# A host that lays x out feature-major and the small vectors as columns, so that the kernel loads x straight into h

## The chip, the cores and the metric

One Trainium2 chip, of which the kernel uses 1 core. The metric is the device time of one execution in microseconds, given as the median of several runs. Beside the timed runs there is one profiled execution, from which all rows below come.

## The reference, cut to what matters

Two transformer blocks run one after the other over 256 tokens of width 2048, all in float32. The first begins like this:

```python
def rmsnorm(x, g):
    x32 = x.astype(jnp.float32)
    y = x32 * lax.rsqrt(jnp.mean(x32 * x32, axis=-1, keepdims=True) + RMS_EPS)
    return (y * g.astype(jnp.float32)).astype(x.dtype)

h = x                                   # (1, 256, 2048)
hn = rmsnorm(h, mix_norm_g[0])
h = h + nsa_mixer(hn, ...)              # 2048 -> 5168 columns, three kinds of attention, 2048 -> 2048
h = h + swiglu(rmsnorm(h, ffn_norm_g[0]))
return rmsnorm(h, final_norm_g)
```

`nsa_mixer` multiplies the normed input by a 2048 x 5168 matrix, compresses keys and values with learned positions (`cmp_pos_k`, `cmp_pos_v`), attends, and projects back. The second block modulates its norms with `silu(c) @ w_mod + b_mod`, attends in two ways and ends in an MLP of width 8192. The norm's vectors, `c`, `b_mod` and the positions are short vectors; everything large is a weight matrix that is read once.

## The kernel before, in words

The residual stream is kept feature-major: tile `h` is 128 partitions x 16 feature blocks x 256 tokens (`KT` = 16, `S` = 256). A norm's 1/rms is a number for each token, so it is never applied to the input of a product: the product takes `x * g`, and its output is scaled by 1/rms when it leaves PSUM.

**Products.** Every float32 operand is split into two numbers of the fp32r type, hi (a rounded copy, ACT) and lo (the remainder, DVE), and each product is three matmuls: hi by hi (line 127), hi by lo (128), lo by hi (129). A `gemm` over 512 columns takes weights in pieces of two feature blocks by 512 columns (512 KB, tile `raw`, 5 buffers, loaded by SP's queue, line 93). ACT makes `whi` from it (line 84), DVE `wlo` (line 85), four buffers each; then TensorE has 24 matmuls of 256 columns on that piece, 12 for each feature block k. So a gemm over 16 blocks is 8 pieces and 192 matmuls. The accumulators are four PSUM banks, two for a gemm of 512 columns, so that the next gemm starts while the last one is being read out.

**Start.** `norm_x` (line 324) issues on SP's queue, in this order: the identity, `mix_norm_g`, and then x in 8 pieces of 256 features (256 KB each, tile `xt`, token-major) with 5 weight pieces among them: x0, w0, x1, w1, x2, x3, w2, x4, x5, w3, x6, x7, w4. Each x piece is turned by four TensorE transposes (line 341) into a PSUM bank; ACT writes `x` hi from that bank with the scale g (line 345), DVE the lo (346), and DVE copies the bank into `h` (348). The squares for the norm are taken from the token-major `xt` by 16 ACT instructions that sum along the row as they go (line 354), into `ssq`; a short DVE and ACT chain makes 1/rms of them (`rstd_x`, line 360). It is needed when the first gemm leaves PSUM (line 421). All other norms sum squares of `h`: `square_sums` (line 645) squares two feature blocks at once on ACT (653), adds them up in `sacc` on DVE (659; the first pair is written into `sacc` itself, the last pair stays in `slast`), and `rstd_col` (236) sums over partitions by six matmuls of one column (line 244). There is one buffer `slast`, so each square waits until DVE has added the one before.

**Vectors.** `columns` (line 218) loads short vectors as rows of 128 numbers and transposes them on TensorE (line 228) into columns, with a DVE copy out of PSUM. It is called for `mix_norm_g`, for seven vectors together (`vectors`, line 277), for the positions (414), and in `mod_cols` (1057) for the modulation and for `b_mod_2`.

**What sets the order.** A planner orders each engine's instructions by a simulated clock: at each point of it, it takes for an engine the ready instruction that comes first in the program. After that each engine runs its list strictly in order and waits at its head for what the next instruction needs. Dependencies are kept for the parts of a tile that an instruction touches. A generator (`self.inner`) emits the squares of `norm_x` one pair after each step of the first gemm, so in program order they stand after the work that feeds that step and before the weight split of the next.

The functions that the change touches:

Of the kernel before, what the change touches and what calls it, by code (L numbers as in the profile page):

```python
# [8 lines left out]
F32 = mybir.dt.float32  # L9
F32R = mybir.dt.float32r  # L10
AF = mybir.ActivationFunctionType
OP = mybir.AluOpType
AX = mybir.AxisListType
# [3 lines left out]
D = 2048  # L17
S = 256
KT = D // 128
# [3 lines left out]
EPS = 1e-6  # L23
# [43 lines left out]
class Kernel:  # L67
# [208 lines left out]

    def vectors(self):
        nc, a, m = self.nc, self.a, self.main
        vec1 = self.columns([(self.vec("ffn_norm_g", 16), 16), (self.vec("final_norm_g", 16), 16),
                             (self.vec("attn_norm_g_2", 16), 16), (self.vec("mlp_norm_g_2", 16), 16),  # L280
                             (self.vec("mla_q_norm_g_2", 3), 3), (self.vec("mla_kv_norm_g_2", 1), 1),
                             (self.vec("c_2", 16), 16)], "vec1")
        self.vecs = {"ffn": vec1[:, 0:16], "final": vec1[:, 16:32], "attn": vec1[:, 32:48],
                "mlp": vec1[:, 48:64], "lat": vec1[:, 64:68]}
        both = self.vecs["both"] = m.tile([128, 16], F32, name="both")
        t = m.tile([128, 16], F32, name="botht", tag="colb", bufs=1)
        nc.vector.tensor_tensor(t, vec1[:, 16:32], vec1[:, 16:32], OP.mult)
        nc.vector.tensor_scalar(t, t, EPS, None, op0=OP.add)
        nc.scalar.activation(both, t, AF.Sqrt)
        nc.vector.reciprocal(both, both)  # L290
        nc.vector.tensor_tensor(t, t, both, OP.mult)
        nc.vector.reciprocal(both, both)
        nc.vector.tensor_tensor(both, both, t, OP.add)
        nc.vector.tensor_scalar(both, both, 0.5, None, op0=OP.mult)
        csil = self.csil = m.tile([128, 16], F32, name="csil")
        nc.scalar.activation(csil, vec1[:, 68:84], AF.Silu)
        self.nsink = m.tile([128, 16], F32, name="nsink")
        nc.gpsimd.dma_start(self.nsink, self.src(a["swa_sinks_2"], 0, [[0, 128], [1, 16]]))
        nc.vector.tensor_scalar(self.nsink, self.nsink, -1.0, None, op0=OP.mult)
# [24 lines left out]
    def norm_x(self):  # L324

        nc, a = self.nc, self.a
        self.gmix = self.columns([(self.vec("mix_norm_g", 16), 16)], "gmix", nc.sync)
        xs = [self.pair("x") for _ in range(KT)]
        xt = []
        for s in range(8):  # L330
            xt.append(self.main.tile([128, 2, S], F32, name="xt", tag="u", bufs=16))
            nc.sync.dma_start(xt[s], self.src(a["x"], s * S, [[D, 128], [128 * D, 2], [1, S]]))
            if s in (0, 1, 3, 5, 7):
                self.ahead.append(self.raw_cols(a["nsa_w_in"], 5168, 256 * len(self.ahead), 2, [(2048, 512)]))
        banks = (("O", 1), ("PT", 1), ("S", 2), ("S", 2))
        for s in range(8):
            p = self.bank(*banks[s % 4])
            k = 2 * s
            for i in range(2):
                for t in range(2):  # L340
                    nc.tensor.transpose(p[:, i * S + t * 128:i * S + (t + 1) * 128],
                                        xt[s][:, t, i * 128:(i + 1) * 128], self.ident)
            for i in range(2):
                g, pi = self.gmix[:, k + i:k + i + 1], p[:, i * S:(i + 1) * S]
                nc.scalar.activation(xs[k + i][:, 0, :], pi, AF.Copy, scale=g)
                nc.vector.scalar_tensor_tensor(xs[k + i][:, 1, :], pi, g, xs[k + i][:, 0, :].bitcast(F32),
                                               op0=OP.mult, op1=OP.subtract)
            nc.vector.tensor_copy(self.h[:, k:k + 2, :].rearrange("p k n -> p (k n)"), p)
        ssq = self.main.tile([128, 2, 8], F32, name="ssq")

        def squares():
            for s in range(8):
                for t in range(2):
                    nc.scalar.activation(self.slast[:, t * S:(t + 1) * S], xt[s][:, t, :], AF.Square,
                                         accum_out=ssq[:, t, s:s + 1])
                yield
        self.inner = squares()
        return xs, ssq

    def rstd_x(self, ssq):  # L360
        for _ in self.inner:
            pass
        rc = self.main.tile([128, 2], F32, name="rc_x")
        self.nc.vector.tensor_reduce(rc, ssq, AX.X, OP.add)
        self.nc.vector.tensor_scalar(rc, rc, 1.0 / D, EPS, op0=OP.mult, op1=OP.add)
        return self.rsqrt(rc, self.main, "rcx")


    def bias_table(self, rel, which, pool):
# [26 lines left out]
    def nsa(self, xs, ssq, mp):  # L396
        nc, a, tc = self.nc, self.a, self.tc
        W, LD = a["nsa_w_in"], 5168
        with ExitStack() as es:
            p = es.enter_context(tc.tile_pool(name="attn", bufs=1))  # L400
# [9 lines left out]
            rc = None  # L410

            with tc.tile_pool(name="cmp", bufs=1) as cp:
                dtab = self.bias_table("rel_bias", 0, cp)
                pos = self.columns([(a["cmp_pos_k"].rearrange("a b c -> (a b) c"), 32),
                                    (a["cmp_pos_v"].rearrange("a b c -> (a b) c"), 32)], "pos")
                ku = cp.tile([128, 2, 32, 60], F32, name="ku")
                for ci in range(2):
                    t = cp.tile([128, 4, S], F32, name="kc", tag="kc", bufs=1)
# [40 lines left out]
                g = cp.tile([128, 2, 48], F32, name="g")  # L459
# [9 lines left out]
                for j, (t, br) in enumerate(((0, 1), (0, 2), (0, 0), (1, 0), (1, 1), (1, 2))):  # L469
                    s = g[:, t, br * 16:(br + 1) * 16]  # L470
# [192 lines left out]
    def sums(self, col, last=2):  # L663
        acc = self.sacc[:, :S]
        self.nc.vector.tensor_tensor(acc, acc, self.sacc[:, S:], OP.add)
        return [(acc, col)] + [(self.slast[:, i * S:(i + 1) * S], col) for i in range(last)]
# [390 lines left out]
    def mod_cols(self, o, n, name):  # L1057

        d = self.modv
        mv = self.columns([(bass.AP(tensor=d.tensor, offset=d.offset + 128 * o, ap=[[128, n], [1, 128]]), n)], name)  # L1060
        bv = self.columns([(self.vec("b_mod_2", n, 128 * o), n)], "b_")
        self.nc.vector.tensor_tensor(mv, mv, bv, OP.add)
        return mv

# [111 lines left out]
_SKIP = ("s5_A_re", "s5_A_im", "s5_log_dt", "s5_B_re", "s5_B_im", "s5_C_re", "s5_C_im", "s5_D", "s5_w_glu")  # L1176


# [13 lines left out]
```

## Time and profile before

| | us |
|---|---|
| median of 3 timed runs | 2123.52 |
| lowest and highest of them | 2122.17, 2125.51 |
| the profiled execution's own time | 2119.85 |
| its span, first to last instruction | 2118.0 |

The span holds 2094.1 us in which the profile counts TensorE (PE) as busy, 1452.0 us of DVE, 1017.1 us of ACT. The ends of matmuls are modelled, so how fast TensorE really goes is read from the distance between the starts of two matmuls, in the timeline.

### The profile page before, as it was taken

What the parts mean: (1) busy time and instruction counts of PE and PEld (TensorE: products, weight loads), DVE (VectorE), ACT (ScalarE), POOL (GpSimd) and SP (SyncE); (2) the same over time, 40 slices, a digit from 0 to 9 for tenths busy, and PEclk for the clock granted to TensorE, in tenths of its full rate; (3) what the DMA queues carried; (4) which work ended last, traced back from release to release, by engine and by line L of the source; (5) the groups of instructions that cost most, each with busy time, mean ns of one, the idle gap of its engine ahead of it and who ended that gap; (6) DMA issues with size and microseconds to landing.
All of it is one profiled execution on the core that took longest, in us unless ns stands there. A gap on an engine that the chain in (4) does not pass through costs nothing. (4 is left out here: it accounts for less than half of the span.)

```text
span 2118.0 us, 40943 instructions
## 1 busy us (share of the span) xinstructions
PE 2094.1 (99%) x16405; PEld 1992.5 (94%) x16405; DVE 1452.0 (69%) x2144; ACT 1017.1 (48%) x1504; POOL 162.9 (8%) x297
## 2 busy tenths in 40 slices
PE   9999999999999999999999999999999999999998
PEld 8899999999999999999999999899889989989987
DVE  7467876787777777877867676677676555555556
ACT  6334655554434434443445465565434534534543
POOL 2211000010110111101000000000100000000000
PEclk9999999999999999999999999999999999999999
DMA  8778555889889888888975663568887656656663
GB/s 277 261 234 311 170 163 180 286 265 296 276 282 303 274 301 281 279 294 276 298 233 156 182 183 112 160 196 280 283 294 233 194 191 194 193 193 193 192 194 133
DMA packets 288302, 492.29 MB, mean 232 GB/s; under 512 B 27111, under 2 KB 139338, under 8 KB 287856
## 3 DMA queue, kind: packets, MB, share of 16 engines
q1 hardware_dynamic: 254128, 371.20, 55.2%
q0 software_dynamic: 33408, 117.70, 16.7%
q8 instruction: 128, 2.10, 0.4%
q10 hardware_dynamic: 576, 0.79, 0.1%
q14 instruction: 62, 0.51, 0.1%
HBM read 487.21 MB, written 2.20 MB: 231 GB/s over the span
## 5 line engine op out<-in xcount | busy, mean ns | idle before, releaser
L84 ACT ACTIVATE whi<-raw 128x1024 fp32r<-128x1024 f32 (+2 forms) x716 | 746.2, 1044 | 904.8 <-PE acc L128 645.4
L85 DVE TENSOR_TENSOR wlo<-raw,whi 128x1024 fp32r<-128x1024 f32 (+2 forms) x716 | 853.5, 1200 | 392.1 <-ACT whi L84 378.8
L127 PE MATMUL acc<-x,whi 128*128 128x256 f32 x3184 | 882.6, 278 | 3.2 <-ACT v L463 1.4
L128 PE MATMUL acc<-x,whi 128*128 128x256 f32 x3184 | 884.3, 278 | 0.0
L129 PE MATMUL acc<-x,wlo 128*128 128x256 f32 x3184 | 882.7, 278 | 0.2 <-DVE wlo L85 0.2
L127 PEld LDWEIGHTS acc<-x,whi 128*128 128x128 f32 x3184 | 597.8, 188 | 8.6 <-issue 5.0
L128 PEld LDWEIGHTS acc<-x,whi 128*128 128x128 f32 x3184 | 599.4, 188 | 5.4 <-issue 4.6
L129 PEld LDWEIGHTS acc<-x,wlo 128*128 128x128 f32 x3184 | 599.0, 188 | 1.4 <-DVE wlo L85 0.6
L742 DVE SCALAR_TENSOR_TENSOR macc<-mw,csil,macc 128x1024 f32<-128x1024 f32 x180 | 231.1, 1284 | 175.0 <-DMA mw<-w_mod 174.1
L128 PE MATMUL acc<-u,whi 128*128 128x256 f32 x1260 | 349.7, 279 | 0.8 <-DVE u L85 0.8
L127 PE MATMUL acc<-u,whi 128*128 128x256 f32 x1260 | 346.3, 280 | 1.0 <-DVE h L642 0.6
L129 PE MATMUL acc<-u,wlo 128*128 128x256 f32 x1260 | 347.0, 278 | 0.0
L128 PEld LDWEIGHTS acc<-u,whi 128*128 128x128 f32 x1260 | 236.7, 188 | 1.9 <-DVE u L85 1.5
L127 PEld LDWEIGHTS acc<-u,whi 128*128 128x128 f32 x1260 | 234.9, 188 | 3.2 <-ACT u L84 1.0
L129 PEld LDWEIGHTS acc<-u,wlo 128*128 128x128 f32 x1260 | 235.9, 188 | 0.7 <-issue 0.2
L164 PE MATMUL acc<-whi,u 128*128 128x512 f32 (+1 forms) x544 | 206.2, 379 | 0.0
L165 PE MATMUL acc<-wlo,u 128*128 128x512 f32 (+1 forms) x544 | 206.1, 379 | 0.0
L163 PE MATMUL acc<-whi,u 128*128 128x512 f32 (+1 forms) x544 | 204.4, 376 | 0.0
L736 POOL DMA_DIRECT2D mw<-w_mod x192 | 102.6, 534 | 1003.2 <-PE acc L129 657.7
L164 PEld LDWEIGHTS acc<-whi,u 128*128 128x128 f32 x544 | 102.2, 188 | 20.6 <-issue 0.4
L163 PEld LDWEIGHTS acc<-whi,u 128*128 128x128 f32 x544 | 102.1, 188 | 20.3
L165 PEld LDWEIGHTS acc<-wlo,u 128*128 128x128 f32 x544 | 102.2, 188 | 18.4
(349 smaller groups left out, 1316.9 us busy)
## 6 DMA issues: line engine op xcount, KB each, us to landing
raw<-w_ff SPq DMA_DIRECT2D x256, 512.0 KB, 4.1
mw<-w_mod POOLq DMA_DIRECT2D x192, 512.0 KB, 5.6
raw<-ffn_w_in SPq DMA_DIRECT2D x352, 256.0 KB, 5.0
raw<-ffn_w_out SPq DMA_DIRECT2D x87, 512.0 KB, 5.3
raw<-nsa_w_in SPq DMA_DIRECT2D x72, 512.0 KB, 5.3
raw<-nsa_w_out SPq DMA_DIRECT2D x32, 512.0 KB, 4.5
raw<-w_out SPq DMA_DIRECT2D x32, 512.0 KB, 4.0
raw<-w_in SPq DMA_DIRECT2D x24, 512.0 KB, 3.9
```

What stands on the lines that cost most here:

```text
L84: self.nc.scalar.activation(hi, x, AF.Copy)
L85: self.nc.vector.tensor_tensor(lo, x, hi.bitcast(F32), OP.subtract)
L127: mm(out, wh, xh, start=first, stop=False, skip_group_check=True)
L128: mm(out, wh, xl, start=False, stop=False, skip_group_check=True)
L129: self.last = mm(out, wl, xh, start=False, stop=last, skip_group_check=True)
L163: mm(o, xt[:, 0, q], hi, start=k == 0, stop=False)
L164: mm(o, xt[:, 1, q], hi, start=False, stop=False)
L165: self.last = mm(o, xt[:, 0, q], lo, start=False, stop=k == nk - 1)
L736: ld = nc.gpsimd.dma_start(wt, self.src(self.a["w_mod_2"], k * 128 * LD + s * 1024, [[LD, 128], [1, 1024]]))
L742: nc.vector.scalar_tensor_tensor(acc, wt, csil[:, k:k + 1], acc, op0=OP.mult, op1=OP.add)
```

## The change

The host passes x transposed (`l_xT`, 2048 x 256), and the short vectors as matrices with 128 rows (`l_gmix`, `l_vec1`, `l_pos`, `l_bmod`). The kernel loads each with one DMA in the shape in which it is used. x goes into `h` in the same 8 pieces, on the same queue, in the same places among the weight pieces. ACT and DVE make x hi and lo from `h`, and the squares go through `square_sums` and `rstd_col`.

```diff
     def vectors(self):
-        vec1 = self.columns([(self.vec("ffn_norm_g", 16), 16), ... (self.vec("c_2", 16), 16)], "vec1")
+        vec1 = m.tile([128, 84], F32, name="vec1")
+        nc.gpsimd.dma_start(vec1, a["l_vec1"])
...
     def norm_x(self):
-        self.gmix = self.columns([(self.vec("mix_norm_g", 16), 16)], "gmix", nc.sync)
+        self.gmix = self.main.tile([128, 16], F32, name="gmix")
+        nc.sync.dma_start(self.gmix, a["l_gmix"])
         xs = [self.pair("x") for _ in range(KT)]
-        xt = []
         for s in range(8):
-            xt.append(self.main.tile([128, 2, S], F32, name="xt", tag="u", bufs=16))
-            nc.sync.dma_start(xt[s], self.src(a["x"], s * S, [[D, 128], [128 * D, 2], [1, S]]))
+            nc.sync.dma_start(self.h[:, 2 * s:2 * s + 2, :],
+                              self.src(a["l_xT"], 256 * s * S, [[S, 128], [128 * S, 2], [1, S]]))
             if s in (0, 1, 3, 5, 7):
                 self.ahead.append(self.raw_cols(a["nsa_w_in"], 5168, 256 * len(self.ahead), 2, [(2048, 512)]))
-        for s in range(8):
-            p = self.bank(*banks[s % 4])
...
-                    nc.tensor.transpose(p[:, i * S + t * 128:i * S + (t + 1) * 128],
-                                        xt[s][:, t, i * 128:(i + 1) * 128], self.ident)
...
-            nc.vector.tensor_copy(self.h[:, k:k + 2, :].rearrange("p k n -> p (k n)"), p)
+        for k in range(KT):
+            g, x = self.gmix[:, k:k + 1], self.h[:, k, :]
+            nc.scalar.activation(xs[k][:, 0, :], x, AF.Copy, scale=g)
+            nc.vector.scalar_tensor_tensor(xs[k][:, 1, :], x, g, xs[k][:, 0, :].bitcast(F32),
+                                           op0=OP.mult, op1=OP.subtract)
+        sums = self.square_sums()
         def squares():
-            for s in range(8):
-                for t in range(2):
-                    nc.scalar.activation(self.slast[:, t * S:(t + 1) * S], xt[s][:, t, :], AF.Square,
-                                         accum_out=ssq[:, t, s:s + 1])
+            for k in range(0, KT, 2):
+                sums(k)
                 yield
...
     def rstd_x(self, _):
         for _ in self.inner:
             pass
-        rc = self.main.tile([128, 2], F32, name="rc_x")
-        self.nc.vector.tensor_reduce(rc, ssq, AX.X, OP.add)
-        self.nc.vector.tensor_scalar(rc, rc, 1.0 / D, EPS, op0=OP.mult, op1=OP.add)
-        return self.rsqrt(rc, self.main, "rcx")
+        return self.rstd_col(self.sums(self.cD[:, 0:1]), EPS, self.main, "rcx")
...
-                pos = self.columns([(a["cmp_pos_k"]..., 32), (a["cmp_pos_v"]..., 32)], "pos")
+                pos = cp.tile([128, 64], F32, name="pos")
+                nc.gpsimd.dma_start(pos, a["l_pos"])
...
-        bv = self.columns([(self.vec("b_mod_2", n, 128 * o), n)], "b_")
+        bv = self.main.tile([128, n], F32, name="bv", tag="colb", bufs=1)
+        self.nc.gpsimd.dma_start(bv, self.a["l_bmod"][:, o:o + n])
```

## Rows read from the trace of the kernel before

**Rows 1.** The page's list of engines: busy us (share of the span), instructions.

```profile
PE 2094.1 (99%) x16405; PEld 1992.5 (94%) x16405; DVE 1452.0 (69%) x2144; ACT 1017.1 (48%) x1504; POOL 162.9 (8%) x297
```

**Rows 2.** Windows: length, busy PE, PEld, DVE, ACT, POOL; clock, DMA share, GB/s.

```profile
5.00:10.00 5.00, 2.02 (x12) 1.78 (x11) 2.79 (x5) 3.78 (x12) 2.48 (x6) 0.80 1.04 308
10.00:15.00 5.00, 5.00 (x39) 5.00 (x39) 2.72 (x4) 3.81 (x12) 1.97 (x4) 0.86 1.08 348
15.00:20.00 5.00, 5.00 (x46) 5.00 (x45) 4.06 (x7) 5.00 (x19) 0.00 (x0) 1.00 1.07 374
...
1150.00:1155.00 5.00, 2.25 (x10) 1.74 (x9) 3.25 (x11) 1.57 (x4) 0.00 (x0) 0.65 0.78 246
```

**Rows 3.** Timeline of PE, first products: start, us, instruction, [idle before].

```profile
8.41 1.12 PE L341 MATMUL PT<-ident,xt 128*128 128x128 f32 x4 [2.98 <-DMA xt<-x]
9.18 0.56 PE L127 MATMUL acc<-x,whi 128*128 128x256 f32 x1
...
9.76 0.41 PE L127 MATMUL acc<-x,whi 128*128 128x256 f32 x1
9.97 0.41 PE L128 MATMUL acc<-x,whi 128*128 128x256 f32 x1
...
13.86 0.36 PE L127 MATMUL acc<-x,whi 128*128 128x256 f32 x1
```

**Rows 4.** Timeline of ACT and DVE: splits of weight pieces 0, 1 and 4.

```profile
6.54 1.06 ACT L84 ACTIVATE whi<-raw 128x1024 fp32r<-128x1024 f32 x1 [0.52 <-DMA raw<-nsa_w_in]
11.03 1.06 ACT L84 ACTIVATE whi<-raw 128x1024 fp32r<-128x1024 f32 x1 [0.98 <-DMA raw<-nsa_w_in]
...
22.23 1.23 DVE L85 TENSOR_TENSOR wlo<-raw,whi 128x1024 fp32r<-128x1024 f32 x1 [0.31 <-ACT whi L84]
```

**Rows 5.** SP's timeline, and DMA issues (last column us to landing): pieces 2, 4.

```profile
4.73 0.92 SPq L93 DMA_DIRECT2D raw<-nsa_w_in  x1
raw<-nsa_w_in SPq DMA_DIRECT2D x1, 512.0 KB, 9.2
...
12.22 0.37 SPq L93 DMA_DIRECT2D raw<-nsa_w_in  x1
raw<-nsa_w_in SPq DMA_DIRECT2D x1, 512.0 KB, 7.5
```

**Rows 6.** Timeline of PE: one group of four transposes among matmuls.

```profile
15.00 0.28 PE L127 MATMUL acc<-x,whi 128*128 128x256 f32 x1
15.12 0.60 PE L341 MATMUL O<-ident,xt 128*128 128x128 f32 x4
15.48 0.37 PE L128 MATMUL acc<-x,whi 128*128 128x256 f32 x1
15.68 0.28 PE L129 MATMUL acc<-x,wlo 128*128 128x256 f32 x1
```

**Rows 7.** Groups by line, 0-45, then 366-446 us; ACT's waits, 360-450: us, times, longest.

```profile
L354 ACT ACTIVATE slast<-xt 128x256 f32<-128x256 f32 x16 | 6.5, 410 | 3.4 <-DMA xt<-x 3.4
L348 DVE COPY h<-S 128x512 f32<-128x512 f32 x4 | 2.7, 681 | 0.0
...
L653 ACT ACTIVATE slast<-h 128x512 f32<-128x512 f32 x7 | 4.4, 630 | 8.1 <-DVE h L642 4.1 <-DVE sacc L659 4.0
...
ACT slast L653 <- DVE sacc L659: 4.0, 4, 1.6
```

**Rows 8.** Timeline of PE: the one-column matmuls of a later norm.

```profile
440.00 0.28 PE L128 MATMUL acc<-x,whi 128*128 128x256 f32 x1
...
440.48 1.03 PE L244 MATMUL S<-cD,slast 128*128 128x1 f32 x8
441.37 0.36 PE L129 MATMUL acc<-x,wlo 128*128 128x256 f32 x1
```

**Rows 9.** Timeline of DVE in the projection after the first attention.

```profile
377.80 1.28 DVE L642 TENSOR_TENSOR h<-h,acc 128x512 f32<-128x512 f32 x2
379.00 0.48 DVE L673 SCALAR_TENSOR_TENSOR x<-h,vec,x 128x256 fp32r<-128x256 f32 x1
```

More of the change, by code (lines that the diff above doesn't have):

```diff
@@ L278, in vectors @@
         nc, a, m = self.nc, self.a, self.main
[L279 to L282, printed above, removed]
+        vec1 = m.tile([128, 84], F32, name="vec1")
+        nc.gpsimd.dma_start(vec1, a["l_vec1"])
         self.vecs = {"ffn": vec1[:, 0:16], "final": vec1[:, 16:32], "attn": vec1[:, 32:48],
@@ L333, in norm_x @@
             if s in (0, 1, 3, 5, 7):
                 self.ahead.append(self.raw_cols(a["nsa_w_in"], 5168, 256 * len(self.ahead), 2, [(2048, 512)]))
-        banks = (("O", 1), ("PT", 1), ("S", 2), ("S", 2))
-        for s in range(8):
-            p = self.bank(*banks[s % 4])
-            k = 2 * s
-            for i in range(2):
-                for t in range(2):
-                    nc.tensor.transpose(p[:, i * S + t * 128:i * S + (t + 1) * 128],
-                                        xt[s][:, t, i * 128:(i + 1) * 128], self.ident)
[L343 to L347, printed above, removed]
-            nc.vector.tensor_copy(self.h[:, k:k + 2, :].rearrange("p k n -> p (k n)"), p)
@@ L349, in norm_x @@
-        ssq = self.main.tile([128, 2, 8], F32, name="ssq")
+        for k in range(KT):
[4 more added lines that the diff above has]
+        sums = self.square_sums()
         def squares():
-            for s in range(8):
-                for t in range(2):
-                    nc.scalar.activation(self.slast[:, t * S:(t + 1) * S], xt[s][:, t, :], AF.Square,
-                                         accum_out=ssq[:, t, s:s + 1])
+            for k in range(0, KT, 2):
+                sums(k)
@@ L356, in squares, with rstd_x @@
                 yield
         self.inner = squares()
-        return xs, ssq
-    def rstd_x(self, ssq):
+        return xs, None
+    def rstd_x(self, _):
         for _ in self.inner:
             pass
-        rc = self.main.tile([128, 2], F32, name="rc_x")
-        self.nc.vector.tensor_reduce(rc, ssq, AX.X, OP.add)
-        self.nc.vector.tensor_scalar(rc, rc, 1.0 / D, EPS, op0=OP.mult, op1=OP.add)
-        return self.rsqrt(rc, self.main, "rcx")
+        return self.rstd_col(self.sums(self.cD[:, 0:1]), EPS, self.main, "rcx")
@@ L413, in nsa @@
                 dtab = self.bias_table("rel_bias", 0, cp)
-                pos = self.columns([(a["cmp_pos_k"].rearrange("a b c -> (a b) c"), 32),
-                                    (a["cmp_pos_v"].rearrange("a b c -> (a b) c"), 32)], "pos")
+                pos = cp.tile([128, 64], F32, name="pos")
+                nc.gpsimd.dma_start(pos, a["l_pos"])
                 ku = cp.tile([128, 2, 32, 60], F32, name="ku")
@@ L1176, with layouts, cols @@
 _SKIP = ("s5_A_re", "s5_A_im", "s5_log_dt", "s5_B_re", "s5_B_im", "s5_C_re", "s5_C_im", "s5_D", "s5_w_glu")
+def layouts(a):
+    def cols(*names):
+        return np.ascontiguousarray(np.concatenate([a.pop(n).reshape(-1, 128).T for n in names], 1))
+    return {"l_xT": np.ascontiguousarray(a.pop("x").reshape(S, D).T), "l_gmix": cols("mix_norm_g"),
+            "l_vec1": cols("ffn_norm_g", "final_norm_g", "attn_norm_g_2", "mlp_norm_g_2", "mla_q_norm_g_2",
+                           "mla_kv_norm_g_2", "c_2"),
+            "l_pos": cols("cmp_pos_k", "cmp_pos_v"),
+            "l_bmod": np.ascontiguousarray(a["b_mod_2"].reshape(-1, 128).T)}
 def kernel(**inputs):
@@ L1185 @@
     arrays.update(constants())
+    arrays.update(layouts(arrays))
     aps = {n: nc.dram_tensor(n, v.shape, mybir.dt.from_np(v.dtype), kind="ExternalInput").ap()
```

## The prediction

> **What bounds the kernel now.** I begin with the page's list of engines: PE counts as busy for 2094.1 of 2118.0 us, DVE for 69% and ACT for 48% [rows 1]. So only two things can move the time: work taken from or given to PE, and the few stretches in which PE is fed too slowly. The change touches the first 40 us, so the second view is the windows of the start: from 5 to 20 us the DMA share is above 1.0 (308 to 374 GB/s), and from 15 to 20 us ACT is full, 5.00 of 5.00 [rows 2]. The third is PE's timeline: it waited 2.98 us for the second x piece and began its first product at 9.18 us; up to about 11.4 us matmuls start 0.21 us apart (9.76, 9.97), later 0.12 (15.00, 15.12) [rows 3, 6]. The fourth is who feeds the products: ACT split weight piece 0 at 6.54 and piece 1 at 11.03, each time right after a wait for its DMA [rows 4]. So the start is set by DMA, ACT and PE in turn, and what a freed PE gains there must be held against when the pieces land.
>
> **What goes from PE.** 32 transposes of x in 8 groups of four. One group in the stream: the matmul at 15.00 is followed by the next at 15.48 and the second next at 15.68, where 0.12 apart would give 15.12 and 15.24, so a group costs 0.44 us [rows 6]. Two of the groups (the first at 4.8 us and the one at 8.41) stand in the start-up wait; two stand together just before 13.86, and four come after it (rows 6 show one of them). The four are worth 4 x 0.44 = 1.8 us; the rest is in the start below. The column transposes of `vec1`, `pos` and `b_mod` go too. At most each costs what a group of four costs (0.44), at least what one of four does (0.11); a single narrow transpose is nearest the lower end, so I take 0.15 each, 0.5 us, range 0.3 to 1.3. The one of `mix_norm_g` lies in the start-up wait and is worth nothing.
>
> **What comes to PE.** Six matmuls of one column, which the trace shows as 12 records: from 440.00 to 441.37 instead of 0.12 later, and the usual 0.08 behind it [rows 8, 6], that is 1.33 us, once, wherever the planner puts it. If they wait there for DVE's last sum, more; that is a rival below.
>
> **The start, step by step.** x0 and piece 0 land as before: the queue order is the same and the bytes are the same; `l_gmix` is the same 8 KB. Without transposes the first product needs x hi and `whi` 0 only: 6.54 + 1.06 = 7.60 us instead of 9.18 [rows 4, 3]. If the clock rises at the same moment, at 11.4, there are 3.8 / 0.21 = 18 matmuls by then and 6 more at 0.12, so the 24 of piece 0 are done at 12.1. Piece 1 lands at 11.03, its `whi` is ready at 12.1, its `wlo` 1.23 later at 13.3. So block 2 starts between 12.1 and 13.1 instead of 13.86 [rows 3, 4]: 0.8 to 1.8 us. Piece 2, issued at 4.73, lands at 13.9, piece 4 at 12.22 + 7.5 = 19.7 [rows 5]. From landing to `wlo` is 1.06 + 1.23 = 2.3 us, and the first matmul that needs it is the third, 0.2 us in: piece 4's block 8 can't go in full before 21.8. Where was it before? From 13.86, six blocks of 12 matmuls at 0.115 (the rows' 0.12, and 0.11 as often) are 8.3 us, four groups of transposes 1.8: 23.9 us, when `wlo` 4 had just been made (22.23 + 1.23 = 23.5 [rows 4]). PE alone would gain 0.8 to 1.8 plus 1.8, so 2.6 to 3.6 us; the landings allow 2.1; and if ACT and DVE hand over piece 4 no earlier than now, 0.4. After piece 4 there is no x left to load and weights come faster than PE eats them, so what is won at block 8 is kept.
>
> **Do ACT and DVE keep up?** ACT loses 16 squares, 6.5 us [rows 7], and gets 8 of 128x512 at 0.63, 5.0 us: 1.5 us less, and the x hi that now read SBUF stay as they are. DVE loses 8 copies of 128x512 at 0.68, 5.4 us, and gets 6 adds of the same shape, for which the copy is the nearest row, 4.1, and one half as wide, 0.4: 0.9 us less. Neither is more loaded. I therefore take the limit of the landings, 2.1 us, and keep 0.4 and 3.6 as ends. The `rstd` chain becomes longer, but 1/rms is wanted only when the first gemm leaves PSUM (13.86 + 14 x 12 x 0.115 + 1.8 = 35 us now), and the second gemm has two other banks and 192 x 0.115 = 22 us of work then: it costs nothing, and the cover is that second gemm.
>
> **The rest.** POOL issues two DMAs for nine in the first 13 us, and one for one near 1082 us; nothing on PE waits for these. The queue of SP has the same DMAs in the same order, so nothing is moved past anything. For `b_mod`, POOL loads it without waiting for PE, and the add that uses it waits for `modv` in any case.
>
> **The sum.** -2.1 - 0.5 + 1.3 = -1.3 us, against the profiled execution's span of 2118.0 (its own time is 2119.85, so 1.85 us lie outside the span and stay). The timed median lies 3.7 us above that execution; the same difference taken from it gives 2123.5 - 1.3 = 2122.2 us, 0.06% less. With the ends: -0.4 - 0.3 + 1.3 = +0.6 and -3.6 - 1.3 + 1.3 = -3.6 us, so 2119.9 to 2124.1 for this case alone. All of it lies within 0.2% (4.2 us), about what a measurement of this kernel can tell from no change.
>
> **Rivals.** *First, the faster one: PE alone sets the start, and the later stretches shift well too.* For it speaks that x lo and hi no longer queue behind transposes, so both engines can work ahead from the landings. It gives -3.6; and the order elsewhere changes, since the planner runs its clock anew. Near 1150 us PE works 2.25 of 5 us at a granted clock of 0.65 [rows 2]: 0.35 x 5 = 1.75 us are lost in that window alone, and a stretch like it may fall better. Together -5.3 us: 2118.2. Against it: piece 4's landing at 19.7.
>
> *Second, slower: squares and adds lock ACT and DVE together.* Each square after the second must wait until DVE has added the one before, as there is one `slast`. Four such waits cost ACT 4.0 us near 420 us [rows 7]. At the start ACT is full from 15 us and DVE nearly, and both run their lists in order; behind a waiting square stand x hi and the next weight split on ACT, for these DVE's lo parts wait, and for both PE. Six waits at 1.0 us are 6.0, less the 1.5 that ACT is relieved and the 0.4 by which `wlo` 4 was early: weight splits come 4.1 us later than now. PE's own savings then only lengthen its waits, and -0.5 + 1.3 stays: +4.9 us, 2128.4. It decides where more than about 2 us of these waits fall before piece 4's split; below that it eats only my gain. Against it: the planner knows the dependency and can put an add early; before, 16 squares stood in the same place.
>
> *Third, x does not come straight: products wait for all of `h`.* If a read of block 0 waited for all eight loads of `h`, the first product would start 9 us later. But DVE wrote two further pairs of `h` at 377.80 before it read the first pair at 379.00 [rows 9], though the program has them the other way round: parts of `h` are told apart. I give it 2%, in the slower share.
>
> *Fourth, the clock.* Until 9.18 PE now has transposes at 4.8 and 8.41 us; afterwards nothing between the warm-up and 7.6. In 5 to 10 us the granted clock is 0.80, in 10 to 15 us 0.86 [rows 2]: (0.20 + 0.14) x 5 / 0.5 = 3.4 us are already at the lower level (1.2 of 2.4 GHz). If the rise comes 2 us later than it does now, 9 matmuls take 0.1 us more each, 0.9 us, though partly under the wait for piece 1: the time is 2122.2 to 2123.1, still the same. The Trainium skill (TensorE: Matmul & The Clock Gate, Part 1: The HAM clock gate) says that the engine is throttled by default and only sustained activity releases it; by that rule the early idle stretch speaks against the change. The trace agrees so far, with 0.80 around the wait of 2.98 us.
>
> **How the numbers follow.** My forecast with the fourth rival 0.58, the first 0.22, the second with the third 0.20. Faster by over 0.2% is the first alone, slower the second and third. The range takes in both: 2117.0 to 2128.0.
>
> **What would show it.** First product at 7.6 to 8 us; block 2 near 13; no L341; 12 records of L244 before 40 us without idle time ahead of them; ACT's waits for L659 in 10 to 25 us below 2 us in all. I am wrong if PE shows waits for `whi` or `wlo` in 12 to 35 us, or waits at L244, or if the stretches near 1150 and 1268 us change by more than the start does.

## The result and the profile after

The changed kernel takes 2206.57 us (median of 4 runs, 2205.49 to 2209.33), the kernel before beside it 2124.52 (2122.17 to 2127.41): ratio 1.0391, 95% interval 1.0378 to 1.0404, some 82 us slower. The profiled execution took 2205.49 us, its span is 2203.7. No case of the prediction held this.

The first line to read is the list of engines, the answer to [rows 1]:

```profile
PE 2178.8 (99%) x16381; PEld 2069.6 (94%) x16381; DVE 1457.3 (66%) x2138; ACT 1012.8 (46%) x1479; POOL 159.2 (7%) x290
```

PE has 24 records fewer and is busy 84.7 us longer, at the same 99%. Its idle time hardly grows (23.9 us of the span before, 24.9 after), so the slowdown is not a wait: the work itself takes longer. A window from the middle of the kernel, which the change does not touch, shows it. First before, then after (columns as in [rows 2]):

```profile
700.00:1140.00 440.00, 439.61 (x3888) 436.72 (x3887) 327.06 (x346) 191.50 (x214) 41.11 (x79) 1.00 0.83 272
```

```profile
700.00:1140.00 440.00, 440.00 (x3679) 437.15 (x3678) 317.75 (x325) 176.74 (x191) 41.36 (x77) 1.00 0.84 268
```

In the same 440 us at the same granted clock PE goes through 209 matmuls fewer. The timeline of PE there, before and after (start, us, instruction):

```profile
900.04 0.28 PE L129 MATMUL acc<-x,wlo 128*128 128x256 f32 x1
900.15 0.28 PE L127 MATMUL acc<-x,whi 128*128 128x256 f32 x1
900.27 0.28 PE L128 MATMUL acc<-x,whi 128*128 128x256 f32 x1
900.38 0.28 PE L129 MATMUL acc<-x,wlo 128*128 128x256 f32 x1
```

```profile
900.04 0.28 PE L129 MATMUL acc<-x,wlo 128*128 128x256 f32 x1
900.16 0.28 PE L127 MATMUL acc<-x,whi 128*128 128x256 f32 x1
900.28 0.28 PE L128 MATMUL acc<-x,whi 128*128 128x256 f32 x1
900.40 0.28 PE L129 MATMUL acc<-x,wlo 128*128 128x256 f32 x1
```

Three steps take 0.34 us before and 0.36 after. Averaged over all neighbouring starts in the two traces (my own count, gaps over 150 ns left out), 256-column matmuls of lines 127 to 129 stand 113.9 ns apart before and 119.9 after. There are 13,332 of them: 6.0 ns each is 80 us. At the end of the first gemm the changed kernel is 1.6 us late, and 191 x 6.0 ns = 1.1 us of that is the new spacing already; so the start, on which nearly all of the prediction was spent, is worth little.

In the code of these matmuls nothing changed. What changed is where their operands lie. Each matmul has a moving operand, 256 columns of `x` or `u` (`u` holds the moving pairs of other gemms), and a stationary one, 128 columns of `whi` or `wlo`. The allocation of the two built programs, in bytes from the start of an SBUF partition (in brackets the remainder modulo 128; it is the same for all buffers of a tile):

```
          x (moving)       u (moving)       whi, wlo (stationary)
before    39200 (mod 128: 32)   71968 (32)    125536, 141920 (96)
after     38176 (32)           124288 (0)      91424, 107808 (32)
```

The change takes `vrows`, the 64-byte tile `ssq` and `pos` from ahead of `whi`, and `u` is first asked for later, so it now lies behind the weights. Of what went from between `x` and `whi`, only the 64 bytes of `ssq` are no multiple of 128. Modulo 128 the stationary operands were 64 bytes from both moving ones; now they are 0 from x and 32 from u. The experiments ask whether that is the cause.

The start, for its share. PE's first products (answer to [rows 3]), and its first waits:

```profile
8.29 0.58 PE L127 MATMUL acc<-x,whi 128*128 128x256 f32 x1 [1.75 <-ACT whi L84]
...
12.91 0.41 PE L128 MATMUL acc<-x,whi 128*128 128x256 f32 x1
13.13 0.36 PE L129 MATMUL acc<-x,wlo 128*128 128x256 f32 x1
13.32 0.28 PE L127 MATMUL acc<-x,whi 128*128 128x256 f32 x1
...
17.15 0.39 PE L127 MATMUL acc<-x,whi 128*128 128x256 f32 x1 [0.44 <-ACT whi L84]
...
18.41 0.39 PE L129 MATMUL acc<-x,wlo 128*128 128x256 f32 x1 [0.52 <-DVE wlo L85]
...
21.74 0.39 PE L127 MATMUL acc<-x,whi 128*128 128x256 f32 x1 [0.68 <-ACT whi L84]
...
23.00 0.38 PE L129 MATMUL acc<-x,wlo 128*128 128x256 f32 x1 [0.52 <-DVE wlo L85]
```

And ACT's timeline there (answer to [rows 4]):

```profile
4.56 1.28 ACT L335 ACT_TABLE_LOAD   x1 [4.56 <-DMA h<-l_xT]
...
7.19 1.04 ACT L84 ACTIVATE whi<-raw 128x1024 fp32r<-128x1024 f32 x1
...
14.64 1.28 ACT L294 ACT_TABLE_LOAD   x1
15.93 0.22 ACT L294 ACTIVATE csil<-vec 128x16 f32<-128x16 f32 x1
16.05 1.04 ACT L84 ACTIVATE whi<-raw 128x1024 fp32r<-128x1024 f32 x1
...
19.23 1.28 ACT L287 ACT_TABLE_LOAD   x1
20.53 0.22 ACT L287 ACTIVATE both<-botht 128x16 f32<-128x16 f32 x1
20.65 1.04 ACT L84 ACTIVATE whi<-raw 128x1024 fp32r<-128x1024 f32 x1
```

The four PE waits from 17 to 23 us, 2.2 us in all, follow the two table loads: each load and the small instruction behind it stand right ahead of a weight split. In the kernel before, `csil` came 46 us later, when its vector had been transposed:

```profile
60.56 1.28 ACT L296 ACT_TABLE_LOAD   x1
61.85 0.22 ACT L296 ACTIVATE csil<-vec 128x16 f32<-128x16 f32 x1
```

### The profile page after: what moved, and what is told of

It reads as the page before. It is cut to its first block, busy times and chain, and to the rows that moved or that the text cites. A ratio compares the mean times of both kernels' runs of the same rounds, so it can differ in the third digit from the quotient of the medians.

```text
span 2203.7 us, 40844 instructions
## 1 busy us (share of the span) xinstructions
PE 2178.8 (99%) x16381; PEld 2069.6 (94%) x16381; DVE 1457.3 (66%) x2138; ACT 1012.8 (46%) x1479; POOL 159.2 (7%) x290
## 5 line engine op out<-in xcount | busy, mean ns | idle before, releaser
L127 PE MATMUL acc<-x,whi 128*128 128x256 f32 x3184 | 903.6, 285 | 5.3 <-ACT whi L84 2.9
L128 PE MATMUL acc<-x,whi 128*128 128x256 f32 x3184 | 905.0, 285 | 0.0
L129 PE MATMUL acc<-x,wlo 128*128 128x256 f32 x3184 | 903.2, 284 | 1.4 <-DVE wlo L85 1.3
L127 PEld LDWEIGHTS acc<-x,whi 128*128 128x128 f32 x3184 | 611.6, 192 | 12.4 <-issue 5.0
L128 PEld LDWEIGHTS acc<-x,whi 128*128 128x128 f32 x3184 | 612.7, 192 | 4.8 <-issue 3.9
L129 PEld LDWEIGHTS acc<-x,wlo 128*128 128x128 f32 x3184 | 612.0, 192 | 3.0 <-DVE wlo L85 2.3
L128 PE MATMUL acc<-u,whi 128*128 128x256 f32 x1260 | 356.3, 284 | 0.8 <-DVE u L85 0.8
L129 PE MATMUL acc<-u,wlo 128*128 128x256 f32 x1260 | 354.0, 283 | 0.0
L127 PE MATMUL acc<-u,whi 128*128 128x256 f32 x1260 | 351.1, 283 | 0.3 <-ACT u L84 0.3
L164 PE MATMUL acc<-whi,u 128*128 128x512 f32 (+1 forms) x544 | 208.3, 383 | 0.0
L163 PE MATMUL acc<-whi,u 128*128 128x512 f32 (+1 forms) x544 | 208.2, 383 | 0.0
```

Of the source, the lines that this page charges most:

```text
L127: mm(out, wh, xh, start=first, stop=False, skip_group_check=True)
L128: mm(out, wh, xl, start=False, stop=False, skip_group_check=True)
L129: self.last = mm(out, wl, xh, start=False, stop=last, skip_group_check=True)
L163: mm(o, xt[:, 0, q], hi, start=k == 0, stop=False)
L164: mm(o, xt[:, 1, q], hi, start=False, stop=False)
```

## The experiments

The theories: **A**, the place of the stationary operand alone; **B**, the distance between stationary and moving operand modulo 128 bytes; **C**, the new order and the squares. In the first seven kernels below and in `a_d64` each engine has the same instructions in the same order as the kernel that they are made from; only addresses differ.

**Moving tiles, nothing else.**

```diff
 b_w64 (from before; b_w32 and b_w96 likewise, with 12 and 20 in place of 16)
-        ssq = self.main.tile([128, 2, 8], F32, name="ssq")
+        ssq = self.main.tile([128, 2, 16], F32, name="ssq")[:, :, 0:8]
 a_w64 (from after): every raw buffer 64 bytes longer
 b_all64 (from before), a_all64 (from after): everything 64 bytes further; b_all96: 96 (32 for 24)
-        ceps = m.tile([128, 2], F32, name="ceps")
+        ceps = m.tile([128, 24], F32, name="ceps")
```

> The kernel before, with 64 bytes more in the dead end of the tile ssq, so that whi and wlo begin at 32 instead of 96 above a multiple of 128 bytes of their partition; x and u stay at 32, and the instructions and their order on every engine are the same. Theory A, the place of the stationary operand alone sets the distance between two 256-column matmuls: it goes from 113 to 120 ns, 13,332 x 0.0067 = 89 us less the stretches that are at 118 now, about 2205 us. Theory B, the distance between the moving and the stationary operand counts (64 bytes apart is fast, 0 is slow): it goes to 0, so also about 2205 us. Theory C, the slowdown comes from the new squares and the new order on ACT and DVE: nothing changes, 2120 to 2127 us at 113 ns.

> The changed kernel, with the five raw buffers 64 bytes longer each, so that whi and wlo begin at 96 above a multiple of 128 bytes, as in the kernel before; x stays at 32, u goes from 0 to 64; same instructions, same order. Theory A: 113 ns, about 2118 to 2125 us. Theory B: x and weights 64 bytes apart, fast; u and weights 32 apart, as now, so 2118 to about 2145 us. Theory C: 2206 us at 120 ns, as the changed kernel.

> The kernel before, with a tile ahead of all large ones 64 bytes longer, so that everything moves by 64 bytes: x and u to 96, whi and wlo to 32 above a multiple of 128; distances between them and the order are as before. Theory A: the weights stand at 32, so 120 ns and about 2205 us. Theory B: distance still 64, so 2120 to 2127 us at 113 ns. Theory C: 2120 to 2127 us.

> The changed kernel, with the same tile 64 bytes longer: x to 96, whi and wlo to 96, u to 64; distances between x and weights stay 0, order as in the changed kernel. Theory A: the weights stand at 96, so 113 ns and about 2118 to 2125 us. Theory B: distance 0 still, so 2206 us at 120 ns. Theory C: 2206 us.

> The kernel before with 32 bytes more behind ssq: x and u at 32, whi and wlo at 0 modulo 128, distance 96. If any distance but 64 is bad: about 120 ns and 2195 to 2210 us. If only distances 0 and 32 are bad: 113 to 118 ns, 2122 to 2148 us.

> The kernel before with 96 bytes more behind ssq: distance 32 for x and u alike. Both theories of the distance expect 120 ns and 2195 to 2210 us, as u at distance 32 had in the changed kernel; a theory in which the absolute place of whi matters (64 here, never tried) could give anything between.

> The kernel before moved by 96 bytes as a whole: distance 64 kept, x and u at 0, whi and wlo at 64 modulo 128. If the distance alone counts: 113 to 118 ns. If the place of x chooses between the two paces (32 gave mostly 113 ns, 96 mostly 118), this tells on which side 0 lies: 2122 to 2128 us or about 2145.

Measured (places modulo 128; time is the median, of one execution for `b_w64`, `a_w64`, `a_all64` and the first `b_all64`, of two for `b_w96` and `b_w32`, of eight for `b_all96`; spacing is my own mean over neighbouring 256-column matmuls, as above; the last column is PE's count in 700 to 1140 us, as in the windows above):

| kernel | x, u, whi | distance x, u | us | ns x, u | matmuls |
|---|---|---|---|---|---|
| before | 32, 32, 96 | 64, 64 | 2122.1 to 2124.5 | 113.8, 114.1 | 3888 |
| after | 32, 0, 32 | 0, 32 | 2206.57 | 119.9, 120.0 | 3679 |
| b_w64 | 32, 32, 32 | 0, 0 | 2195.04 | 119.1, 118.7 | 3720 |
| b_w96 | 32, 32, 64 | 32, 32 | 2205.65 | 120.0, 119.9 | 3677 |
| b_w32 | 32, 32, 0 | 96, 96 | 2182.17 | 118.0, 118.1 | 3743 |
| a_w64 | 32, 64, 96 | 64, 32 | 2158.17 | 114.6, 119.9 | 3805 |
| a_all64 | 96, 64, 96 | 0, 32 | 2205.25 | 119.9, 119.9 | 3679 |
| b_all64 | 96, 96, 32 | 64, 64 | 2145.27 | 115.9, 116.2 | 3747 |
| b_all96 | 0, 0, 64 | 64, 64 | 2121.97 | 114.0, 113.7 | 3885 |

`b_w64` is the kernel before with 64 idle bytes in it, and it is 70 us slower. Its window, to be held against the two above:

```profile
700.00:1140.00 440.00, 440.00 (x3720) 437.14 (x3720) 322.46 (x335) 179.18 (x194) 41.55 (x78) 1.00 0.83 270
```

A falls: whi at 32 is slow in `b_w64` and not in `b_all64`, whi at 96 slow in `a_all64` and fast in before. C falls as the cause of the 82 us, since the order is the same. B holds: every kernel at distance 64 has 114 to 116 ns whatever the absolute places, every other distance 118 to 120, and `a_w64`, where x is at 64 and u is not, has each at its own pace (its 2158 us lie above the 2145 expected at most). The expectation for `b_w32` that any distance but 64 costs the full 6 ns was too strong: 96 costs 4.

**The two paces at distance 64.** There the stream stands at 113.3 ns in some stretches and at 117.8 in others, and goes over from one to the other at an interruption. `b_all64` again, unchanged:

> The kernel of b_all64 again (before, moved by 64 bytes as a whole), in several executions. It showed 2145 us once, with 118 ns for most of the long stretches. If its place makes the higher pace: all executions near 2145. If each execution falls into one of the two paces by chance: executions spread from 2118 to 2150, most of them like before's.

Ten executions lie between 2120.99 and 2145.68, median 2124.26. So the first 2145.27 was no effect of the place; executions of one program fall into different shares of the two paces. The two traces of this one program show it: long stretches at 117.8 ns prevail in the one of 2145.27, those at 113.3 in the one of 2124.61. That chance takes up to some 20 us of any single execution; two of `b_all96` (2136.33, 2142.95), of which no trace was kept, fit it.

**The change at distance 64.**

```diff
 a_d64 (from after)
-        raw = self.main.tile([128, kk, n], F32, name="raw", tag="raw", bufs=5)
+        raw = self.main.tile([128, kk * n + 16], F32, name="raw", tag="raw", bufs=5)[:, 0:kk * n].rearrange("p (k n) -> p k n", n=n)
-        v = pool.tile([128, 2], F32, name=name + "v")
+        v = pool.tile([128, 26 if name == "rcx" else 2], F32, name=name + "v")[:, 0:2]
```

> The changed kernel with its instructions and their order untouched, and two paddings (64 bytes behind each raw buffer, 96 behind a small tile), so that x and u again lie 64 bytes (modulo 128) from whi and wlo, as in the kernel before. If the distance is the whole cause, the matmuls are 113 to 118 ns apart again and the time is 2118 to 2127 us with the lower pitch throughout, up to 2148 with the higher one; the blind sum's -1.3 us (or +5) is then what the change itself does. If the changed order of the start or of the squares takes part of the 82 us, the time stays above 2150.

2128.19 us (12 runs) against 2122.12 of before (23 runs), ratio 1.0031 (1.0019 to 1.0043). The padding gives back 78 of the 84 us by which the two medians, 2206.57 and 2122.12, differ. What is left, about 6.6 us (4 to 9), is the change's own, and two kernels with one part each divide it.

```diff
 v_only: before, with vec1, pos and b_mod loaded as columns from l_vec1, l_pos, l_bmod (as in the change)
 x_d64: after, with vec1, pos and b_mod through columns() as before, and
+        self.main.tile([128, 2, 8], F32, name="ssq")
         sums = self.square_sums()
   and the longer v of a_d64
```

> One part of the change alone: the vectors as columns (vec1, pos, b_mod), while x is loaded and transposed as before. Its whi lies 64 modulo 128 from x and u without any padding. Theory of the distance: about 113 to 114 ns between matmuls, so 2118 to 2128 us, never near 2206. If the vectors' early arrival is what costs in the start (Silu and Sqrt tables loaded on ACT among the first weight splits, 2 x 1.28 us), products reach the end of the first gemm 1 to 3 us later than before; if it costs nothing, within 0.5 us.

> The other part alone: x and mix_norm_g from the host, squares through square_sums; vec1, pos and b_mod by column transposes as before. The tile ssq is kept, unused, and 96 bytes are added behind a small tile, so that x and u lie 64 from the weights. The blind sum without the vectors' part (-2.1 + 1.3 = -0.8 us) gives 2121 to 2123 if the start goes as predicted without table loads; if the squares lock ACT and DVE together (the second rival), 2126 to 2130; if the start is as late as in the whole change at distance 64 (first gemm's end +0.6 us), the table loads were not its cause.

`v_only`: 2126.89 (11 runs), ratio 1.0017 (1.0002 to 1.0032). `x_d64`: 2120.84 (12 runs), ratio 0.9991 (0.9980 to 1.0002), against 2123.22 of before. When the k-th product matmul starts, against the kernel before (us, one trace each):

```
product           0     48     96    191    383    960   1500   1575   8000   13300
a_d64         -0.80  -0.81  +1.14  +0.64  +0.96  -0.35  -0.48  +3.03  +3.16  +6.39
v_only        -0.54  +1.11  +2.71  +3.59  +3.15  +1.73  +1.73  +3.51  +8.33  +7.13
x_d64         -0.85  -0.34  -1.05  -2.11  -1.79  -3.11  -1.98  -2.10  +2.44  +0.91
```

The part of x gains 1.8 us by the end of the second gemm (product 383), the vectors lose 3.15: their tables load in the start, at 13.14 and 16.01 us in `v_only`, and not before 58 us in `x_d64`. So the vectors' early arrival costs the 3 us. That it does so by the table loads is read from the order of ACT and PE's waits above; no run left the vectors early and took the loads away. The squares do not lock ACT and DVE together: in the changed kernel ACT waited once for an add in its start.

```profile
ACT slast L637 <- DVE sacc L643: 1.2, 1, 1.2
```

Over whole executions the two parts alone, +3.6 us and -1.9, make 1.7 of the 6.6; the trace of `a_d64` shows where more goes. Its step of 3.5 us between products 1500 and 1575 begins with a wait far from the start. PE and DVE in it, then DVE before:

```profile
315.98 0.72 PE L572 MATMUL S<-kT,qT 128*128 128x271 f32 x2 [1.67 <-DVE qT L474]
...
314.04 1.28 DVE L726 SCALAR_TENSOR_TENSOR macc<-mw,csil,macc 128x1024 f32<-128x1024 f32 x1 [4.72 <-DMA mw<-w_mod]
315.24 1.28 DVE L474 TENSOR_TENSOR qT<-acc,rq 128x512 f32<-128x512 f32 x2
```

```profile
312.11 1.29 DVE L742 SCALAR_TENSOR_TENSOR macc<-mw,csil,macc 128x1024 f32<-128x1024 f32 x1 [2.32 <-DMA mw<-w_mod]
```

DVE stands at its head for a piece of `w_mod` that lands 1.9 us later, `qT` is queued behind it, and PE waits 1.67 us. The other half of the step is the clock: right behind the wait, from 317.0 to 320.5 us, the granted clock is 0.51 in `a_d64` and 1.00 before, so half of 3.4 us is lost, 1.7 us. `v_only` waits 1.5 us there at a granted clock of 1.00, and its step is 1.8. The later differences I put down to the two paces (between 1100 and 1190 us `a_d64` runs at 117.8 ns, before at 113.3), which is chance by the runs of `b_all64r`; no run separates it from a further effect.

**The version that the runs point to**: `x_d64` with pos and b_mod from the host.

> The version the runs point to: the change without its part for vec1 (column transposes as before, so that the Silu and Sqrt tables load later), pos and b_mod as columns from the host, x and u kept 64 from the weights by the unused ssq and 96 bytes behind a small tile. x_d64 gave 0.9991 of before; the two column transposes taken out are worth about 0.3 us, so 2120 to 2122 us where before is 2123, ratio 0.998 to 1.000. If the order near 310 us falls as in v_only and a_d64 (DVE waiting for a piece of w_mod ahead of qT), 3 us more.

2121.96 (12 runs), ratio 0.9998 (0.9985 to 1.0012) against 2123.61: no different from before. Its products are 2.16 us early at 383, where `a_d64`, with the early vec1, is 0.96 late; at 1575 they are 0.94 late, so the stretch near 310 us, where PE again waits for `qT` (2.2 us), took the gain.

**TensorE alone.** Four kernels of such matmuls and none of the reference's other work.

> The disputed cost by itself; it computes nothing of the reference. Matmuls of the same shape and type (128x128 stationary, 256 columns moving, fp32r, hi-hi, hi-lo, lo-hi on four blocks) in 64 groups of 72, with nothing else running: moving operands at 0, 32, 64, 96 (xa to xd), stationary at 0, 16, ..., 112 (wa to wh) modulo 128, each pair twice. If TensorE's own two reads decide by their distance: about 113 (or 118) ns where stationary minus moving is 64, about 120 at 0 and 32, about 118 at 96, the same for all four places of x; the 16-byte steps were never seen. If the effect comes from the writes of ACT and DVE or from DMA, all 64 groups show one pace. If the absolute place counts, rows of the same distance differ.

> As micro (it computes nothing of the reference), with moving operands at 32 modulo 128 only, stationary at 0, 16, ..., 112, and ahead of each of 96 groups of 72 matmuls one short matmul of 8 to 192 columns into another bank, which shifts the stream. In micro an undisturbed stream kept one pace for each pair of places, 116.7 to 120.1 ns, and 117.8 at distance 64. If distance 64 is special because only there a second, faster cadence of 113 ns exists, into which a disturbance can drop the stream: at 64 (wg) some of the twelve groups run at 113.3 and others at 117.8, at the other distances none runs below 116. If the faster cadence exists at every distance, groups at 113 turn up at several. If it needs the other engines' work, no group is below 116.

> As micro2 (it computes nothing of the reference), with the kinds of disturbance behind which the full kernel's stream changed its pace, ahead of 96 groups in turn: two float32 matmuls with a one-column stationary operand, two float32 matmuls of one column, a wait for ACT's reading of the accumulator, a float32 matmul of 128 columns. If distance 64 is special because a cadence of 113 ns exists only there: some groups at wg (distance 64) at 113.3, none at another distance below 116. If 113 ns needs the other engines' work, no group is below 116.

With one moving pair and four blocks of weights used over and over, the spacing in `micro` is 116.7 to 120.0 ns, the same in both rounds. Distance 64 gives 117.8 at all four places of x and is not the fastest. Against the expectation, other distances differ with the place of x: 0 gives 118.6 to 120.0, 32 gives 118.2 or 120.0, 96 gives 116.7 to 118.7. The built addresses sort nearly all of this modulo 256: there 0 gives 119.7 and 120.0, 128 gives 118.6; 32 gives 118.2, 160 gives 120.0; 64 and 192 both give 117.8. The kernels above agree: x is at 0 modulo 256 in after (119.9), at 128 in `b_w64` (119.1). All kernels that I call distance 64 are at 64 modulo 256; whether 192 is as fast in the full kernel was not tried. Interruptions (`micro2`, `micro3`) move the pace at some other distances too, at 112 between 117.4 and 119.9, at 48 between 117.8 and 123.1, but 113 never appears. So these missed what the kernel before has.

```diff
 micro4 (against micro3)
-    the same moving pair for every k, weights in one 4 KB block
+    xs[k] for k in 0..15, weights 2 KB further with every k (four steps, then again), wlo 8 KB behind whi
+    in the second half: 150 x (DMA of 512 KB, ACT and DVE split), read by nothing on PE
```

> As micro3 (it computes nothing of the reference), but each group is a gemm as in the full kernel: 192 matmuls that walk through 16 moving pairs and through weights 2 KB apart. Moving at 32 modulo 128; stationary at 0, 32, 64, 96 (wa, wc, we, wg: distances 96, 0, 32, 64), each four times with the other engines silent, then four times while SP loads 512 KB pieces and ACT and DVE split them. If the walk through the operands makes the 113 ns cadence possible: 113.3 at wg in the silent half already. If the other engines' work does: at wg in the second half alone. In both cases none below 116 at wa, wc, we. If 113 appears nowhere, what opens it in the full kernel stays open.

Groups by line, operands and shape of line 56, all eight groups of a distance together (96, 0, 32, 64 for wa, wc, we, wg; the mean is the time that one matmul takes, which overlaps with the next, and not the spacing):

```profile
L56 PE MATMUL acc<-xb,wc 128*128 128x256 f32 x512 | 144.9, 283 | 0.0
...
L56 PE MATMUL acc<-xb,we 128*128 128x256 f32 x512 | 144.6, 282 | 0.0
...
L56 PE MATMUL acc<-xb,wa 128*128 128x256 f32 x512 | 143.3, 280 | 0.0
...
L56 PE MATMUL acc<-xb,wg 128*128 128x256 f32 x512 | 141.4, 276 | 0.0
```

And its timeline at distances 0 and 64:

```profile
425.08 0.28 PE L56 MATMUL acc<-xb,wc 128*128 128x256 f32 x1
425.20 0.28 PE L57 MATMUL acc<-xb,wc 128*128 128x256 f32 x1
425.32 0.28 PE L55 MATMUL acc<-xb,wc 128*128 128x256 f32 x1
425.44 0.28 PE L56 MATMUL acc<-xb,wc 128*128 128x256 f32 x1
...
470.14 0.28 PE L57 MATMUL acc<-xb,wg 128*128 128x256 f32 x1
470.25 0.28 PE L55 MATMUL acc<-xb,wg 128*128 128x256 f32 x1
470.37 0.28 PE L56 MATMUL acc<-xb,wg 128*128 128x256 f32 x1
470.48 0.28 PE L57 MATMUL acc<-xb,wg 128*128 128x256 f32 x1
```

Past the first dozen matmuls of a group the spacing is 117.3 ns at 96 (118.7 in one group of eight), 120.0 at 0, 120.0 at 32, 113.3 at 64, in the silent half as beside the loads and splits (DMA share 0.92 to 0.95 from 400 to 600 us). So the price is there with TensorE alone; the other engines have no part in it. As nothing but addresses differs, I put it down to TensorE's reading of its two operands; no run looks inside that. Which part of the walk opens the 113 ns was not tried.

## Why the prediction was wrong

**The step that failed** is in the prediction's first paragraph: "only two things can move the time: work taken from or given to PE, and the few stretches in which PE is fed too slowly". There is a third, the pace of a matmul, which every term took from rows of before (0.12 or 0.115 us apart) as if it belonged to the shape. It depends on where two tiles lie. "So nothing is moved past anything" was true of the queues and false of SBUF: the diff takes three small tiles from ahead of the weights and moves the first use of `u`. That tiles move could be read from the diff; what it costs stood in no row of before. The missing term is 13,332 x 6.0 ns = 80 us of the 82. The profile had a warning: matmuls of one shape stood 0.12 us apart in one place [rows 6] and 0.11 as often, so the shape alone did not set the pace, and I averaged the two.

**POOL's loads**: "nothing on PE waits for these" failed. PE does not wait for `vec1`, but the order of ACT hangs on it: the vector no longer waits for a transpose, so what is made of it, `csil` and `both`, went into the start, and each brought a table load of 1.28 us in among the weight splits. That is the 3 us of `v_only`. A rule that the prediction did not use bears on it: the Trainium skill (ScalarE: Activation LUTs, What ACT_TABLE_LOAD costs) gives 1283 ns for a load, and the trace agrees with 1.28 us. The page adds a drain of about 1380 ns to each switch; these rows show none, as `csil` starts 1.29 us after its load.

**The start.** First product 8.29 us, not 7.6. The wait of ACT's first instruction for `h` now has the first table load behind it (at 4.56 us; at 0.74 before), and a square of 0.6 us stands ahead of the split, which therefore ends at 8.23. Block 2 at 13.67, not 12.1 to 13.1: matmuls stay 0.21 us apart until 13.13, in the kernel before until 11.25. That is the fourth rival as it stood, about 2 us later, 0.9 us: 12.1 + 0.7 + 0.9 = 13.7. The windows, the answer to [rows 2], seem to speak against the clock, with 1.00 where before had 0.80 and 0.86:

```profile
5.00:10.00 5.00, 3.11 (x8) 1.52 (x9) 3.08 (x6) 4.54 (x8) 1.60 (x3) 1.00 1.00 267
10.00:15.00 5.00, 5.00 (x32) 5.00 (x32) 4.13 (x9) 3.76 (x7) 0.00 (x0) 1.00 0.99 342
```

But a window reads 1.00 where the trace has no record of the clock. The first record of the changed kernel is full speed (2.4 GHz) at 13.28 us, where the spacing falls to 0.12; in the kernel before a record of half speed (1.2 GHz) ends at 11.42, where it falls there. So it was the clock, 1.9 us later. That the change made it late is not shown: with the order of before it rose at 11.27 us in `b_all64r` and at 13.91 in `b_w64`. Nor was PE idle up to the first product, as the rival has it: a product for the bias table, 1.43 us long, stands at 5.10.

What the runs agree with: with the tables away (`x_d64`) the sum of x's part, -2.1 + 1.3 = -0.8, measured -1.8 at product 383 and -2.4 us in the median (interval -4.2 to +0.4).

**The one-column matmuls** were right: 12 records, no wait ahead, and 38.80 - 37.42 - 0.12 + 0.07 = 1.33 us, as [rows 8] gave.

```profile
37.42 0.28 PE L129 MATMUL acc<-x,wlo 128*128 128x256 f32 x1
37.54 0.50 PE L244 MATMUL S<-cD,sacc 128*128 128x1 f32 x4
37.90 1.03 PE L244 MATMUL S<-cD,slast 128*128 128x1 f32 x8
38.80 0.36 PE L127 MATMUL acc<-x,whi 128*128 128x256 f32 x1
```

**The rivals.** The first had the wrong sign. The second named the right sign for a wrong reason: one wait of 1.2 us, where it needed 6.0; its own 2128.4 us also lay 0.4 above a range that was said to take it in. The third is out, since the first product comes before most of `h` has landed. The end of the prediction said what would refute it: PE waiting for `whi` in 12 to 35 us, which it does, and far stretches changing by more than the start, as the window from 700 to 1140 us does.

## What to carry to other kernels

When the rate of a matmul changes in stretches that a change does not touch, compare where its operands lie before looking for waits; a tile added, dropped or asked for in another place moves everything behind it. Here 64 bytes that nothing reads were worth 3%. For a stream of such gemms (fp32r, 256 columns), start by trying the stationary operand 64 bytes (modulo 256) from the moving one, which was the fastest of the distances 0, 32, 64 and 96 tried here, and test a change at the same distance, or its own effect (here +0.3%) drowns in the layout's (+3.9%). A load that arrives earlier is not free either: what it makes ready may be put ahead of what the bottleneck waits for.

## What the runs showed of the hardware

The spacing of back-to-back fp32r matmuls of 256 columns depends on the distance between stationary and moving operand, modulo 128: 113.3 or 117.8 ns at 64, 117 to 119 at 96, 118 to 120 at 0 and 32. Within the last two, the remainder modulo 256 tells the values apart (0 and 160: 119.7 to 120.0; 32 and 128: 118.2 to 119.1). The Trainium skill (TensorE: Matmul & The Clock Gate, Step-by-step: what each phase is for) says that TensorE has two independent SBUF read ports and that loading the next weights takes no read bandwidth from the running matmul; by that rule the distance would not matter, and `micro4`, in its first half with no other reader, shows 6.7 ns between distance 0 and 64. The measurement decides. At distance 64 there are two paces, and an interruption can carry the stream from one to the other; what decides which was not found. With one moving pair and the same weights over and over (`micro`) only the slower one was seen, so the gain of distance 64 needs the walk of a gemm.
